# Lengths of k and q from ScalarE's accumulator, and masks made from ScalarE's sign

## The chip, the core and the metric

The kernel runs on one core of a Trainium2 chip. The metric is the device time of one execution in microseconds, as the median of several runs. The core has five engines with a queue of instructions each: TensorE (PE; its weight loads are listed apart as PEld), VectorE (DVE), ScalarE (ACT), GpSimd (POOL) and SyncE (SP, which here issues the DMAs). Each engine takes its instructions strictly in order, and semaphores let one wait for another.

## The reference, cut to what matters

One layer over 1024 tokens of 1024 features: a mixer of two head groups, then an MLP. The change touches two places of the mixer.

The sparse attention keeps, for every query, the 256 keys with the highest score among those it may see, with the earlier key first among equals:

```python
score = jnp.where(key_pos[None, None, :] < limit[None, :, None], score, -jnp.inf)
_, idx = lax.top_k(score, topk)          # topk = 256
```

The DeltaNet group (4 heads of 128) scales every query and key to unit length before its chunked recurrence:

```python
def l2_norm(x):
    return xf * lax.rsqrt(jnp.sum(xf * xf, axis=-1, keepdims=True) + EPS)
q = l2_norm(q.reshape(B, T, B_HEADS, B_HEAD_DIM))
k = l2_norm(k.reshape(B, T, B_HEADS, B_HEAD_DIM))
```

## The kernel before, in words

The program is written as generators (`scoring`, `bisect`, `projections`, `chain`, `levels`, ...) that a planner, `Flow`, interleaves by assumed costs, and the framework's own scheduler then sets the order in which instructions stand in each engine's queue. So an edit in one place can move instructions in others. The stage that matters here lies at about 185 to 427 us of the span. In it run side by side:

- **The projections.** TensorE multiplies the normed input with columns of `w_in` (L199 to L201, the tiles `two`). For q, k and v of the DeltaNet, `conv` follows: a scaled copy on ScalarE (L587), three multiply-adds on VectorE (L589), a Silu on ScalarE (L592).
- **The DeltaNet heads.** When q and k of a head are there, `delta_head` (called four times, for h = 0 to 3) turns them with TensorE (L684, four 128x128 blocks into a PSUM bank, four such banks a head). Of each bank it squares the four blocks (L686 on ScalarE), copies the two of k (L687), and sums the squares per row (L688 on VectorE) into `nr`, a column for every length. From `nr` come the inverse lengths (L691, then the steps L212 to L217) and the factors of the head (L694 to L698); L705 and L706 make the chunk matrices `la`.
- **`base_blocks`.** When the chunk matrices of all heads are stored (`la_d`), this inverts their 32x32 diagonal blocks on VectorE in 31 pairs of steps (L725, L726) and a copy (L727). A store (`tu_d`, L728) and eight loads (`dt`, L740) follow; GpSimd makes `ui` and `te` from `dt` (L783), and the first level of the recurrence goes through TensorE, ScalarE and VectorE (L797, L798, L806, L807, L810, L812, L822, L823, L831, L838, L839).
- **The bisection.** `bisect` finds the threshold of the 256 best scores of each query for six blocks of 128 queries, bit by bit: 31 further bits after the first. In every bit ScalarE counts three blocks (sign and accumulator, L521, widths 1024, 768 and 640), VectorE counts the other three (L528, widths 896, 512 and 384), and VectorE makes the next candidate `cand` of all six from the counts (L531, L532, L533). A sign count of the next bit waits for L533, and L532 waits for the counts of both engines.
- **The masks.** When the thresholds `thr` are there (L540 to L559), each block gets its mask: ScalarE takes the sign of threshold minus score with its sum `sg` (L567), VectorE marks the scores equal to the threshold (L570), counts them along the row (L571, a scan), works out how many are needed (L574, L575), keeps the first of them (L576), adds the greater ones (L577) and writes 0 or a large negative number to `maskb` (L578). The tile `jk`, of two buffers, holds ScalarE's signs and the marks.
- **The end of the stage.** `post_c` scales the latent rows `c_row` (L432 to L437), the last steps of it on VectorE. TensorE turns `c_row` (L1098), and attention and the recurrence begin.

Of the kernel before, what the change touches and what calls it, by code (L numbers as in the profile page):

```python
# [8 lines left out]
F32 = mybir.dt.float32  # L9
F32R = mybir.dt.float32r  # L10
BF16 = mybir.dt.bfloat16
I32 = mybir.dt.int32
AF = mybir.ActivationFunctionType
OP = mybir.AluOpType
AX = mybir.AxisListType
# [3 lines left out]
P = 128  # L19
T = 1024  # L20
# [6 lines left out]
NEG = -2.0 ** 100  # L27
# [112 lines left out]
def block_kernel(ctx: ExitStack, tc: tile.TileContext, x, w_in, c_norm, w_uk, w_uv, rel_bias, conv_w, a_log,  # L140
# [4 lines left out]
    V, S, G, PE, SY = nc.vector, nc.scalar, nc.gpsimd, nc.tensor, nc.sync  # L145
    pl = Pools(tc)
# [141 lines left out]
    ps = psw()  # L288
# [15 lines left out]
    ps = pst()  # L304
# [3 lines left out]
    for half in range(2):  # L308
# [9 lines left out]
        for k in range(NK):  # L318
            ps = psx()
            for j in range(4):  # L320
# [4 lines left out]
                                   op0=OP.mult, op1=OP.subtract)  # L325
# [23 lines left out]
    maskb = pl.t(msk, [P, sum(w_of(b) for b in range(NB))], BF16, "maskb")  # L349
    moff = [sum(w_of(i) for i in range(b)) for b in range(NB)]  # L350
# [14 lines left out]
    ph, ph_close = pl.open("ph")  # L365
# [128 lines left out]
    def bisect():  # L494
        yield "scored"

        cand = pl.t(ph, [P, 6], I32, "cand")
        bare = pl.t(ph, [P, 6], I32, "bare")  # L500
        cnt = pl.t(ph, [P, 6], F32, "cnt")
        lim = pl.t(ph, [P, 6], F32, "lim")
        t01 = pl.t(ph, [P, 6], I32, "t01")
        V.memset(cand, 0)
        for i, b in enumerate(DVB):
            G.memset(lim[:, i:i + 1], P * (b + 1) - TOPK + 0.5)
        for i, b in enumerate(ACB):
            G.memset(lim[:, 3 + i:4 + i], float(P * (b + 1) - 2 * TOPK + 1))


        top = {b: pl.t(ph, [P, P * (b + 1)], BF16, f"top{b}") for b in DVB}
        for b in DVB:
            G.tensor_copy(top[b], s_of(b).bitcast(BF16)[:, 1::2])
        for bit in range(31, -1, -1):
            flip = (1 << bit) ^ (1 << (bit - 1)) if bit else 1
            ta = td = flow.now
            for i, b in enumerate(ACB):
                n = P * (b + 1)
                ta = act(ta, n / 1200 + 0.45)
                junk = pl.t(ph, [P, T], BF16, "jk", bufs=2)  # L520
                S.activation(junk[:, :n], s_of(b), AF.Sign, bias=cand[:, 3 + i:4 + i].bitcast(F32), scale=-1.0,  # L521
                             accum_out=cnt[:, 3 + i:4 + i])
            for i, b in enumerate(DVB):
                n = P * (b + 1)
                td = dve(td, n / 960 + 0.28)
                junk = pl.t(ph, [P, T], BF16, "pre")
                sb = s_of(b) if bit < 16 else top[b]
                V.tensor_scalar(junk[:, :n], sb, cand[:, i:i + 1].bitcast(F32), None, op0=OP.is_lt, op1=OP.add,  # L528
                                accum_out=cnt[:, i:i + 1])
            if bit < 31:  # L530
                V.tensor_scalar(bare, cand, flip, None, op0=OP.bitwise_xor)  # L531
                V.tensor_tensor(t01, cnt, lim, OP.is_le)  # L532
                V.scalar_tensor_tensor(cand, t01, bit, bare, op0=OP.logical_shift_left, op1=OP.bitwise_xor)  # L533
            else:

                V.tensor_tensor(t01, cnt, lim, OP.is_gt)
                V.tensor_scalar(t01, t01, -1.0, None, op0=OP.mult)
                V.tensor_scalar(cand, t01, 1 << 30, None, op0=OP.bitwise_xor)
            yield dve(max(ta, td), 0.8)
        V.tensor_copy(thr[:, 0:3], cand[:, 0:3].bitcast(F32))  # L540


        t = cand[:, 3:6].bitcast(F32)
        up = pl.t(ph, [P, 3], F32, "up")
        least = pl.t(ph, [P, 3], F32, "least")
        for i, b in enumerate(ACB):
            n = P * (b + 1)
            j1 = pl.t(ph, [P, T], BF16, "jk", bufs=2)
            V.tensor_scalar(j1[:, :n], s_of(b), t[:, i:i + 1], None, op0=OP.is_gt, op1=OP.add,
                            accum_out=up[:, i:i + 1])  # L550
            j2 = pl.t(ph, [P, T], BF16, "jk", bufs=2)
            V.tensor_scalar(j2[:, :n], s_of(b), t[:, i:i + 1], BIG, op0=OP.is_le, op1=OP.mult)
            V.tensor_tensor_reduce(out=j2[:, :n], in0=j2[:, :n], in1=s_of(b), scale=1.0, scalar=BIG, op0=OP.add,
                                   op1=OP.min, accum_out=least[:, i:i + 1])
            yield dve(flow.now, 3 * n / 960 + 0.6)
        pick = pl.t(ph, [P, 3], I32, "pick")
        V.tensor_scalar(pick, up, TOPK - 0.5, None, op0=OP.is_ge)
        V.tensor_copy(thr[:, 3:6], t)
        V.copy_predicated(thr[:, 3:6], pick, least)  # L559

        for b in range(NB - 1, 1, -1):
            i = (DVB + ACB).index(b)
            n = P * (b + 1)
            sb, th = s_of(b), thr[:, i:i + 1]
            j1 = pl.t(ph, [P, T], BF16, "jk", bufs=2)
            sg = pl.t(ph, [P, 1], F32, "sg", bufs=2)
            S.activation(j1[:, :n], sb, AF.Sign, bias=th, scale=-1.0, accum_out=sg)  # L567
            eq = pl.t(ph, [P, T], BF16, "jk", bufs=2)
            pre = pl.t(ph, [P, T], mybir.dt.float16, "pre")
            V.tensor_scalar(eq[:, :n], sb, th, None, op0=OP.is_equal)  # L570
            V.tensor_tensor_scan(pre[:, :n], eq[:, :n], eq[:, :n], 0.0, op0=OP.add, op1=OP.max)  # L571

            need = pl.t(ph, [P, 1], F32, "need", bufs=2)
            V.tensor_tensor(need, sg, pre[:, n - 1:n], OP.add)  # L574
            V.tensor_scalar(need, need, 0.5, TOPK - 0.5 * n, op0=OP.mult, op1=OP.add)  # L575
            V.scalar_tensor_tensor(eq[:, :n], pre[:, :n], need, eq[:, :n], op0=OP.is_le, op1=OP.mult)  # L576
            V.scalar_tensor_tensor(eq[:, :n], sb, th, eq[:, :n], op0=OP.is_gt, op1=OP.add)  # L577
            V.tensor_scalar(maskb[:, moff[b]:moff[b] + n], eq[:, :n], -NEG, NEG, op0=OP.mult, op1=OP.add)  # L578
            yield dve(act(flow.now, n / 1200 + 0.4), 5.5 * n / 960 + 1.0)
        flow.done("topk", flow.now)  # L580

# [22 lines left out]
    H4 = [P, 4, P]  # L604

    def v4(ps):
        return ps.rearrange("p (h c) -> p h c", c=P)
# [67 lines left out]
    def delta_head(h, kqh):  # L675

        eh = pl.t(dna, [P, NB, P], F32, "eh")
        SY.dma_start(eh, e_d[h])
        nr = pl.t(dna, [P, NB, 2], F32, "nr")
        kr = pl.t(dna, [P, NB, P], F32, "kr")  # L680
        for n in range(0, NB, 2):
            ps = psx()
            for i in range(4):
                PE.transpose(ps[:, i * P:(i + 1) * P], kqh[:, n + i // 2, i % 2, :], ident)  # L684
            sq = pl.t(dna, H4, F32, "e", bufs=2)
            S.activation(sq, v4(ps), AF.Square)  # L686
            S.copy(kr[:, n:n + 2, :], v4(ps)[:, 0:4:2])  # L687
            V.tensor_reduce(nr[:, n:n + 2, :].rearrange("p n a -> p (n a)"), sq, axis=AX.X, op=OP.add)  # L688
        SY.dma_start(kr_d[:, :, h, :].rearrange("n t d -> t n d"), kr)
        n2 = nr.rearrange("p n a -> p (n a)")  # L690
        V.tensor_scalar(n2, n2, EPS, None, op0=OP.add)  # L691
        r = rsqrt(dna, n2, 16, "rn").rearrange("p (n a) -> p n a", a=2)
        f2 = sm("f2")[:, :, h]
        V.tensor_mul(f2, r[:, :, 0], r[:, :, 0])  # L694
        V.tensor_mul(f2, f2, sm("beta")[:, :, h])
        V.tensor_mul(sm("nk")[:, :, h], nr[:, :, 0], r[:, :, 0])
        V.tensor_mul(sm("k2")[:, :, h], f2, sm("eg")[:, 1, :, h])
        V.tensor_scalar(sm("rq")[:, :, h], r[:, :, 1], 128 ** -0.5, None, op0=OP.mult)  # L698
        for n in range(NB):
            if n % 4 == 0:  # L700
                la = pl.t(dna, [P, 4, 2, P], F32, "la", bufs=2)
            if n % 2 == 0:
                ps = psx()
            o = ps[:, (n % 2) * 256:(n % 2) * 256 + 256]
            PE.matmul(o, kqh[:, n, 0, :], kqh[:, n].rearrange("p a c -> p (a c)"), start=True, stop=True)  # L705
            V.scalar_tensor_tensor(la[:, n % 4], o.rearrange("p (a c) -> p a c", a=2), sm("f2")[:, n, h:h + 1],  # L706
                                   eh[:, n, None, :].to_broadcast([P, 2, P]), op0=OP.mult, op1=OP.mult)
            if n % 4 == 3:
                SY.dma_start(la_d.rearrange("s (n h) a c -> s n h a c", h=4)[:, n - 3:n + 1, h], la)
# [240 lines left out]
    dna = dn = dn2 = at = None  # L950
# [624 lines left out]
    while ready:  # L1575
# [4 lines left out]
        ps = bank_[{2: 1, 3: 5, 4: 7}.get(j, j)]  # L1580
# [225 lines left out]
```

## Time and profile before

| | |
|---|---|
| median of 3 runs | 1376.51 us (1376.21 to 1377.81) |
| profiled execution | 1379.91 us, of which the span is 1378.2 us |
| TensorE busy | 1280.1 us (93%) |
| VectorE busy | 1111.6 us (81%) |
| ScalarE busy | 738.0 us (54%) |
| GpSimd busy | 226.1 us (16%) |
| chain of waits, by engine | PE 66%, DVE 21%, DMA 5%, ACT 4%, issue 2% |

The busy shares are means over stages with different limits. A duration in a timeline runs from the start of an instruction to its end, and the next one on the same engine often starts a little before that end; what an instruction takes of its queue is the distance between two starts. In the chain of waits, "issue" is time in which an engine waited for nothing that the profile shows.

### The profile page before, as it was taken

What the parts mean: (1) busy time and instruction counts of PE and PEld (TensorE: products, weight loads), DVE (VectorE), ACT (ScalarE), POOL (GpSimd) and SP (SyncE); (2) the same over time, 40 slices, a digit from 0 to 9 for tenths busy, and PEclk for the clock granted to TensorE, in tenths of its full rate; (3) what the DMA queues carried; (4) which work ended last, traced back from release to release, by engine and by line L of the source; (5) the groups of instructions that cost most, each with busy time, mean ns of one, the idle gap of its engine ahead of it and who ended that gap; (6) DMA issues with size and microseconds to landing.
All of it is one profiled execution on the core that took longest, in us unless ns stands there. A gap on an engine that the chain in (4) does not pass through costs nothing.

```text
span 1378.2 us, 20181 instructions
## 1 busy us (share of the span) xinstructions
PE 1280.1 (93%) x6628; PEld 1107.6 (80%) x6628; DVE 1111.6 (81%) x2557; ACT 738.0 (54%) x1549; POOL 226.1 (16%) x257
## 2 busy tenths in 40 slices
PE   7899998897977999988989799999999899999996
PEld 5678886776766999978878688888887688888885
DVE  4665679998998899996677467788777978888897
ACT  6555456677614767776455456566656333243422
POOL 1113231221243444349110000000000000000000
PEclk9999999899988999999999999999999999999998
DMA  6223224454255332324455825665567976736215
GB/s 196 78 92 92 62 81 118 137 145 100 69 122 161 95 110 86 95 89 151 152 183 185 295 74 197 213 213 197 202 214 243 393 239 224 248 113 221 78 42 187
DMA packets 184146, 213.33 MB, mean 155 GB/s; under 512 B 28161, under 2 KB 123626, under 8 KB 183914
## 3 DMA queue, kind: packets, MB, share of 16 engines
q1 hardware_dynamic: 184042, 212.06, 47.6%
q8 instruction: 52, 0.85, 0.3%
q14 instruction: 52, 0.43, 0.1%
HBM read 138.58 MB, written 75.00 MB: 155 GB/s over the span
## 4 chain that ended last, share of the span: by engine, by line
PE 66%; DVE 21%; DMA 5%; ACT 4%; issue 2%; SPq 1%; DVEq 0%; ACTq 0%
PE sc L199 4%; PE acc L199 4%; PE sc L200 4%; PE acc L200 4%; PE sc L201 4%; PE acc L201 4%; PE ch L199 4%; PE ch L200 4%; PE ch L201 4%; PE two L199 3%; PE two L200 3%; PE two L201 3%; DVE pre L528 3%; PE tr L199 2%; PE tr L200 2%
## 5 line engine op out<-in xcount | busy, mean ns | idle before, releaser
L199 PE MATMUL two<-hTH,wh 128*128 128x512 f32 (+1 forms) x416 | 166.0, 400 | 22.7 <-ACT tmp L409 14.3
L200 PE MATMUL two<-hTL,wh 128*128 128x512 f32 (+1 forms) x416 | 163.3, 392 | 0.3 <-DVE hTL L324 0.3
L201 PE MATMUL two<-hTH,wl 128*128 128x512 f32 (+1 forms) x416 | 163.0, 393 | 0.0
L521 ACT ACTIVATE jk<-score,cand 128x1024 bf16<-128x1024 f32 (+2 forms) x96 | 92.4, 963 | 52.5 <-DVE cand L533 41.0
L199 PEld LDWEIGHTS two<-hTH,wh 128*128 128x128 f32 (+1 forms) x416 | 80.7, 194 | 39.3 <-issue 18.8
L201 PEld LDWEIGHTS two<-hTH,wl 128*128 128x128 f32 (+1 forms) x416 | 80.9, 194 | 12.9 <-issue 0.5
L200 PEld LDWEIGHTS two<-hTL,wh 128*128 128x128 f32 (+1 forms) x416 | 80.9, 194 | 12.7 <-DVE hTL L324 0.9
L1426 ACT CAST hl<-raw 128x512 fp32r<-128x512 f32 x81 | 48.5, 614 | 70.1 <-PE acc L200 48.7
L1426 ACT CAST hl<-tt 128x512 fp32r<-128x512 f32 x56 | 34.4, 616 | 69.0 <-PE tr L200 39.5
L269 POOL TENSOR_TENSOR wl<-stg,wh 128x1024 fp32r<-128x1024 f32 x23 | 54.7, 2376 | 81.1 <-ACT wh L266 63.7
L1426 ACT CAST hl<-tmp 128x512 fp32r<-128x512 f32 x60 | 35.8, 618 | 55.9 <-DVE tmp L1543 30.3
L1162 ACT ACTIVATE big<-big,nm 128x256 f32<-128x256 f32 (+6 forms) x64 | 50.6, 791 | 22.1 <-DVE nm L1161 18.4
L1427 DVE TENSOR_TENSOR hl<-raw,hl 128x512 fp32r<-128x512 f32 x81 | 55.2, 685 | 5.2 <-ACT hl L1426 2.8
L1188 DVE TENSOR_TENSOR part<-tr,part 128x512 fp32r<-128x512 f32 x80 | 50.3, 631 | 7.3 <-ACT part L1187 7.1
L1210 PE MATMUL acc<-part,VS 128*128 128x256 f32 x288 | 50.0, 297 | 4.1 <-DVE part L1188 4.0
L1187 ACT CAST part<-tr 128x512 fp32r<-128x512 f32 x80 | 42.7, 540 | 16.2 <-PE tr L1185 15.4
L589 DVE SCALAR_TENSOR_TENSOR tmp<-two,svT,tmp 128x1023 f32<-128x1023 f32 (+2 forms) x36 | 45.9, 1276 | 6.3 <-ACT tmp L587 6.3
L199 PE MATMUL acc<-h2H,hl 128*128 128x512 f32 x120 | 46.6, 390 | 3.9 <-ACT tmp L1477 3.9
L479 DVE SCALAR_TENSOR_TENSOR score<-ch,wab,score 128x512 f32<-128x512 f32 (+3 forms) x40 | 26.0, 655 | 28.1 <-ACT ch L478 27.8
L1185 PE MATMUL tr<-ident,big 128*128 128x128 f32 x288 | 46.1, 276 | 2.8 <-DVE part L1188 2.1
L1138 POOL TENSOR_TENSOR mt<-tz,maskb 128x256 f32<-128x256 f32 x56 | 37.9, 682 | 64.0 <-DVE mx L1154 48.3
L268 POOL TENSOR_SCALAR wh<-stg 128x1024 fp32r<-128x1024 f32 x19 | 19.9, 1049 | 170.2 <-PE two L200 156.3
(514 smaller groups left out, 4103.9 us busy)
## 6 DMA issues: line engine op xcount, KB each, us to landing
hid<-tmp SPq DMA_DIRECT2D x140, 256.0 KB, 2.4
hq<-hid SPq DMA_DIRECT2D x80, 256.0 KB, 5.2
raw<-in_w_mlp_in_dram SPq DMA_DIRECT2D x14, 1024.0 KB, 5.7
tmp<-hid SPq DMA_DIRECT2D x56, 256.0 KB, 5.4
raw<-in_w_mlp_out_dram SPq DMA_DIRECT2D x13, 1024.0 KB, 7.4
stg<-in_w_in_dram SPq DMA_DIRECT2D x25, 512.0 KB, 4.0
x<-in_x_dram SPq DMA_DIRECT2D x8, 512.0 KB, 5.4
la_d<-la SPq DMA_DIRECT2D x8, 512.0 KB, 3.0
```

The costliest lines, as they stand in the source:

```text
L199: PE.matmul(o, lh, rh, start=start, stop=False, skip_group_check=more)
L200: PE.matmul(o, lh, rl, start=False, stop=False, skip_group_check=more)
L201: PE.matmul(o, ll, rh, start=False, stop=stop, skip_group_check=more)
L269: (V if early else G).tensor_sub(wl[:, :, :n], f[:, :, :n], wh[:, :, :n].bitcast(F32))
L521: S.activation(junk[:, :n], s_of(b), AF.Sign, bias=cand[:, 3 + i:4 + i].bitcast(F32), scale=-1.0, accum_out=cnt[:, 3 + i:4 + i])
L589: V.scalar_tensor_tensor(acc[:, 3 - j:T], both[:, 0:T - 3 + j], w[j], acc[:, 3 - j:T], op0=OP.mult, op1=OP.add)
L1162: S.activation(pr[:, :n], pr[:, :n], AF.Exp, bias=nm, accum_out=den[:, hh:hh + 1])
L1185: PE.transpose(ps[:, c * P:(c + 1) * P], u["p"][hh][:, (j + a) * P:(j + a + 1) * P], ident)
L1188: V.tensor_sub(pt[:, 0:2 * nj, 1, :], v4(ps)[:, 0:2 * nj], pt[:, 0:2 * nj, 0, :].bitcast(F32))
L1210: PE.matmul(po[:, hh * 256:hh * 256 + 256], VS[:, j + a, 2 * p + hh, :], pt[:, 2 * a + hh].rearrange("p a t -> p (a t)"), start=j + a + hh ...
L1426: S.copy(h_, src)
L1427: eng.tensor_sub(l_, src, h_.bitcast(F32))
```

## The change

In the masks, ScalarE's sign is written into the mask's own place in `maskb` (bf16) instead of a `jk` tile. VectorE's test for equality (L570) and its comparison (L577) read that sign and compare it with the constant 0, where they read the fp32 scores and compared with the threshold of each row.

In `delta_head`, ScalarE squares each 128x128 block in an instruction of its own and sums it per row in its accumulator, straight into `nr`; the wide square and VectorE's reduction go. The copy of k stands ahead of the squares. The new squares are on L688, the copy on L685.

```diff
             n = P * (b + 1)
             sb, th = s_of(b), thr[:, i:i + 1]
-            j1 = pl.t(ph, [P, T], BF16, "jk", bufs=2)
+            mk = maskb[:, moff[b]:moff[b] + n]
             sg = pl.t(ph, [P, 1], F32, "sg", bufs=2)
-            S.activation(j1[:, :n], sb, AF.Sign, bias=th, scale=-1.0, accum_out=sg)
+            S.activation(mk, sb, AF.Sign, bias=th, scale=-1.0, accum_out=sg)
             eq = pl.t(ph, [P, T], BF16, "jk", bufs=2)
             pre = pl.t(ph, [P, T], mybir.dt.float16, "pre")
-            V.tensor_scalar(eq[:, :n], sb, th, None, op0=OP.is_equal)
+            V.tensor_scalar(eq[:, :n], mk, 0.0, None, op0=OP.is_equal)
...
             V.scalar_tensor_tensor(eq[:, :n], pre[:, :n], need, eq[:, :n], op0=OP.is_le, op1=OP.mult)
-            V.scalar_tensor_tensor(eq[:, :n], sb, th, eq[:, :n], op0=OP.is_gt, op1=OP.add)
-            V.tensor_scalar(maskb[:, moff[b]:moff[b] + n], eq[:, :n], -NEG, NEG, op0=OP.mult, op1=OP.add)
+            V.scalar_tensor_tensor(eq[:, :n], mk, 0.0, eq[:, :n], op0=OP.is_lt, op1=OP.add)
+            V.tensor_scalar(mk, eq[:, :n], -NEG, NEG, op0=OP.mult, op1=OP.add)
...
                 PE.transpose(ps[:, i * P:(i + 1) * P], kqh[:, n + i // 2, i % 2, :], ident)
-            sq = pl.t(dna, H4, F32, "e", bufs=2)
-            S.activation(sq, v4(ps), AF.Square)
             S.copy(kr[:, n:n + 2, :], v4(ps)[:, 0:4:2])
-            V.tensor_reduce(nr[:, n:n + 2, :].rearrange("p n a -> p (n a)"), sq, axis=AX.X, op=OP.add)
+            for i in range(4):
+                sq = pl.t(dna, [P, P], BF16, "e", bufs=2)
+                S.activation(sq, ps[:, i * P:(i + 1) * P], AF.Square, accum_out=nr[:, n + i // 2, i % 2:i % 2 + 1])
```

The order of the queues changes with it. The first piece is ScalarE's queue in head 1, before: the sign counts of one bit (L521, to the first of the next bit) with the wide squares (L686, into `e`) and the copies of k (L687).

```order
L521 ACTIVATE jk_2292,cnt_1245<-score_357,cand_1243 128x1024
L521 ACTIVATE jk_2294,cnt_1245<-score_357,cand_1243 128x768
L686 ACTIVATE e_1678<-tr_1673 128x512
L687 COPY kr_1654<-tr_1673 128x256
L521 ACTIVATE jk_2296,cnt_1245<-score_357,cand_1243 128x640
L686 ACTIVATE e_1687<-ch_1682 128x512
L687 COPY kr_1654<-ch_1682 128x256
L521 ACTIVATE jk_2665,cnt_1245<-score_357,cand_1243 128x1024
```

After, ScalarE's queue in the same head, from the last count of one bit to the first of the next, with the narrow squares (L688) between.

```order
L521 ACTIVATE jk_2376,cnt_1245<-score_357,cand_1243 128x640
L688 ACTIVATE e_1695,nr_1673<-ch_1689 128x128
L688 ACTIVATE e_1697,nr_1673<-ch_1689 128x128
L688 ACTIVATE e_1699,nr_1673<-ch_1689 128x128
L688 ACTIVATE e_1701,nr_1673<-ch_1689 128x128
L688 ACTIVATE e_1709,nr_1673<-tr_1703 128x128
L688 ACTIVATE e_1711,nr_1673<-tr_1703 128x128
L688 ACTIVATE e_1713,nr_1673<-tr_1703 128x128
L688 ACTIVATE e_1715,nr_1673<-tr_1703 128x128
L688 ACTIVATE e_1723,nr_1673<-ch_1717 128x128
L688 ACTIVATE e_1725,nr_1673<-ch_1717 128x128
L521 ACTIVATE jk_2745,cnt_1245<-score_357,cand_1243 128x1024
```

Where one wide square stood between two counts, ten narrow ones stand now.

The second place is VectorE's queue at the end of `base_blocks`. Before, its last steps and the copy L727 stand within the last bit of the bisection:

```order
L725 TENSOR_TENSOR kqh_2186<-kqh_2181 128x31
L528 TENSOR_SCALAR pre_3528,cnt_1245<-score_357,cand_1243 128x384
L726 TENSOR_TENSOR kqh_2181<-kqh_2181,kqh_2186 128x31
L532 TENSOR_TENSOR t_207_1247<-cnt_1245,lim_1246 128x6
L727 COPY kqh_2181<-kqh_2181 128x1024
L533 SCALAR_TENSOR_TENSOR cand_1243<-t_207_1247,bare_1244 128x6
```

After, VectorE's queue has them within the second mask (that of width 896):

```order
L725 TENSOR_TENSOR kqh_2266<-kqh_2261 128x31
L570 TENSOR_SCALAR jk_3661<-maskb_340 128x768
L575 TENSOR_SCALAR need_3653<-need_3653 128x1
L726 TENSOR_TENSOR kqh_2261<-kqh_2261,kqh_2266 128x31
L576 SCALAR_TENSOR_TENSOR jk_3649<-pre_3650,need_3653,jk_3649 128x896
L727 COPY kqh_2261<-kqh_2261 128x1024
L577 SCALAR_TENSOR_TENSOR jk_3649<-maskb_340,jk_3649 128x896
```

The copy moved from ahead of the last threshold to behind the first mask and half of the second.

The third place is VectorE's queue where the first level of the recurrence stands. Before, L807 stands among the masks:

```order
L570 TENSOR_SCALAR jk_3597<-score_357,thr_365 128x640
L807 TENSOR_SCALAR te_2707<-ch_2850 32x4x32
L577 SCALAR_TENSOR_TENSOR jk_3584<-score_357,thr_365,jk_3584 128x768
L571 SCALAR_TENSOR_TENSOR pre_3598<-jk_3597 128x640
L578 TENSOR_SCALAR maskb_340<-jk_3584 128x768
```

After, VectorE's queue has the whole level and the scaling of `c_row` (from L434) behind the last mask:

```order
L577 SCALAR_TENSOR_TENSOR jk_3697<-maskb_340,jk_3697 128x384
L578 TENSOR_SCALAR maskb_340<-jk_3697 128x384
L807 TENSOR_SCALAR te_2787<-ch_2930 32x4x32
L812 TENSOR_SCALAR ui_2785<-ch_2930 32x4x32 x2
L831 TENSOR_TENSOR vk_2786<-ch_2971,sm_nk_1502 128x512
L839 TENSOR_SCALAR ui_2785<-ch_3040 64x4x64
L434 TENSOR_SCALAR css_2986<-css_2986 128x8
L212 TENSOR_SCALAR cr_u_3009<-css_2986 128x8
```

The level's four steps moved from between the masks to behind them all.

## Rows read from the trace of the kernel before

**Rows 1.** Busy us and instructions by engine in three stretches; PEclk is the granted clock.

```profile
185.00:310.00 125.00, 114.03 (x520) 96.29 (x519) 118.11 (x309) 84.85 (x163) 29.72 (x22) 0.95 0.45 128
310.00:375.00 65.00, 55.09 (x243) 46.54 (x242) 60.74 (x177) 44.47 (x97) 17.17 (x10) 0.95 0.30 78
375.00:425.00 50.00, 34.22 (x167) 28.35 (x165) 48.46 (x82) 11.87 (x31) 17.72 (x11) 0.82 0.55 134
```

**Rows 2.** Waits from 180 to 425 us: total us, times, longest.

```profile
ACT jk L521 <- DVE cand L533: 41.0, 24, 4.1
...
DVE t L532 <- ACT jk L521: 1.8, 6, 0.5
```

**Rows 3.** Timeline in head 0: start us, us, engine, line, operation.

```profile
187.51 0.59 ACT L686 ACTIVATE e<-tr 128x512 f32<-128x512 f32 x1
187.99 0.38 ACT L687 COPY kr<-tr 128x256 f32<-128x256 f32 x1
...
188.17 0.68 DVE L688 TENSOR_REDUCE nr<-e 128x4 f32<-128x512 f32 x1
188.76 0.74 DVE L528 TENSOR_SCALAR_CACHE_REDUCE pre<-top,cand 128x512 bf16<-128x512 bf16 x1
```

**Rows 4.** Narrow squares elsewhere: timeline (PSUM), and groups with mean ns (SBUF).

```profile
416.44 0.28 ACT L432 ACTIVATE c_row<-ch 128x128 f32<-128x128 f32 x1 [0.28 <-PE ch L429]
...
416.71 0.27 ACT L432 ACTIVATE c_row<-ch 128x128 f32<-128x128 f32 x1
...
L927 ACT ACTIVATE sq<-o 128x128 bf16<-128x128 f32 x32 | 9.6, 302 | 4.1 <-DVE o L907 2.1 <-DVE o L909 1.9
L927 ACT ACTIVATION_READ_ACCUMULATOR sq<-o 128x1 f32 x32 | 6.0, 189 | 0.0
```

**Rows 5.** One bit of the bisection in the timeline; two groups of VectorE.

```profile
197.79 1.15 ACT L521 ACTIVATE jk<-score,cand 128x1024 bf16<-128x1024 f32 x1 [3.66 <-DVE cand L538]
...
200.58 0.19 ACT L521 ACTIVATION_READ_ACCUMULATOR jk<-score,cand 128x1 f32 x1
...
202.36 2.38 POOL L269 TENSOR_TENSOR wl<-stg,wh 128x1024 fp32r<-128x1024 f32 x1
...
202.42 2.34 DVE L533 SCALAR_TENSOR_TENSOR cand<-t,bare 128x6 int32<-128x6 int32 x1
...
L528 DVE TENSOR_SCALAR_CACHE_REDUCE pre<-score,cand 128x896 bf16<-128x896 f32 (+2 forms) x48 | 39.8, 829 | 0.2
...
L726 DVE TENSOR_TENSOR kqh<-kqh,kqh 128x31 f32<-128x31 f32 (+15 forms) x31 | 12.2, 392 | 0.1
```

**Rows 6.** The masks on VectorE in the timeline.

```profile
384.33 0.75 DVE L570 TENSOR_SCALAR jk<-score,thr 128x1024 bf16<-128x1024 f32 x1
385.12 2.29 DVE L571 TENSOR_TENSOR_SCAN pre<-jk 128x1024 f16<-128x1024 bf16 x1
...
401.11 0.61 DVE L570 TENSOR_SCALAR jk<-score,thr 128x768 bf16<-128x768 f32 x1
...
405.02 1.02 DVE L576 SCALAR_TENSOR_TENSOR jk<-pre,need,jk 128x768 bf16<-128x768 f16 x1
...
406.85 1.02 DVE L577 SCALAR_TENSOR_TENSOR jk<-score,thr,jk 128x768 bf16<-128x768 f32 x1
...
409.19 0.33 DVE L578 TENSOR_SCALAR maskb<-jk 128x768 bf16<-128x768 bf16 x1
```

**Rows 7.** Timeline from the end of `base_blocks` to the end of the stage.

```profile
375.19 1.08 DVE L727 COPY kqh<-kqh 128x1024 f32<-128x1024 f32 x1
376.19 0.15 DVE L533 SCALAR_TENSOR_TENSOR cand<-t,bare 128x6 int32<-128x6 int32 x1
...
386.00 5.91 POOL L783 TENSOR_TENSOR ui<-dt,bd 128x512 f32<-128x512 f32 x3 [19.67 <-DMA dt<-tu_d]
...
393.30 1.97 PE L797 MATMUL ch<-te,lo 128*128 128x64 f32 x8 [3.59 <-POOL te L783]
...
426.71 1.97 PE L1098 MATMUL tr<-ident,c_row 128*128 128x128 f32 x8 [6.53 <-DVE c_row L437]
```

## The prediction

> **What bounds the kernel now.** I read three views, in this order. The table of stretches comes first: between 185 and 425 us the reader sees VectorE busy for 118.1 of 125 us, then 60.7 of 65, then 48.5 of 50, while ScalarE is busy for 84.9, 44.5 and 11.9 and TensorE for 114.0, 55.1 and 34.2 [rows 1]. Both edits of this change lie in these 240 us. VectorE has 12.7 us without work in them. Then the waits of the same stretch: ScalarE stood idle 41.0 us for VectorE's next threshold (L533), and VectorE only 1.8 us for ScalarE's counts (L532) [rows 2]. So VectorE sets the pace, and the loop between the two engines is not closed tightly. Last, the end of the stage: TensorE stands still until c_row is written by VectorE (L437) and starts the attention part at 426.71 [rows 7]. I call that moment the stage's end. I take what moves it to move the program's end by as much, since nothing later can begin without it.
>
> The frame: the profiled execution took 1379.91 us (a span of 1378.2 and 1.7 around it), 3.4 above the median of 1376.51. I sum differences within the trace and apply them to the median.
>
> **The change part by part.**
>
> *The reductions that go.* Sixteen of them, 0.68 us each; one started at 188.17 and the next instruction on VectorE at 188.76, so each takes 0.59 us of the queue [rows 3]. 16 x 0.59 = 9.4 us: 2.4 in head 0, which lies ahead of the bisection's first threshold, and 7.1 in heads 1 to 3.
>
> *The squares that come.* A wide square took 0.48 us of ScalarE's queue (187.51 to 187.99 [rows 3]); four narrow ones with an accumulator replace it. The trace has no such operation in this place, but two like it: on a 128x128 block of PSUM the next one started 0.27 us later (416.44, 416.71), and from SBUF one takes 0.30 and its accumulator 0.19 [rows 4], which overlap to about 0.30 a pair. I take 0.28, near the PSUM one, since the new squares read PSUM, and keep 0.27 to 0.33 for the range. 64 x 0.28 - 16 x 0.48 = 17.9 - 7.7 = 10.2 us more for ScalarE. By the stretches alone ScalarE has that room. The question is whether it has it at the right places.
>
> *The places: round by round.* The bisection has 31 bits. In each ScalarE runs three sign counts, 2.98 us from the first start to the last accumulator (197.79 to 200.77 [rows 5]), and VectorE three counts (mean 0.83) and three small steps, some 2.8 us net of overlaps [rows 5]; neither can start the next bit without the other. What else stands in either queue within a round is read from the order. I priced every round so, each instruction at the spacing of its rows, and took the longer queue. Before, ScalarE's is the longer in 6 of 30 rounds, by 3.8 us in all. After, it is in 11, by 14.8 us: squares stand in bundles between two counts, up to 12 in a round (one such piece is shown above: 10 squares, 2.8 us, after a count, and the next count behind them), and the heads' later steps (L691 on) fall behind, so that VectorE's queue holds rounds of almost nothing but counts in between. VectorE's own sum falls from 158.1 to 144.1: 7.1 for the reductions, and the rest for steps of base_blocks that now stand behind the last bit: 17 steps at about 0.32 (rows of 0.39 less an overlap of 0.08 [rows 5]) and the copy L727 (1.0), 6.4 us in all. So the longer queues sum to 158.1 + 3.8 = 161.9 before and 144.1 + 14.8 = 158.9 after: the last bit ends 3.0 us earlier, not 14. Head 0 adds about 1.0: it loses 2.4 on VectorE, but the conv's copy (L587) now waits behind two more narrow squares on ScalarE, and VectorE waits for that. Both orders pay as well for GpSimd: L533 at 202.42 took 2.34 us and ended with GpSimd's L269, 202.36 to 204.74 [rows 5]. There are 13 such pairs, and I leave them equal. So the last threshold, 376.34 before [rows 7], comes at 372.3.
>
> *The masks.* The equality test read fp32 scores: 0.61 us at 768 columns. A tensor_scalar from bf16 to bf16 at that width took 0.33 (L578) [rows 6]. Scaled over the six widths (4224 columns) that saves 0.28 x 4224 / 768 = 1.5 us. The comparison L577 keeps its time: L576, whose operands have 16 bits each, took 1.02 us at 768 columns, as L577 with fp32 did [rows 6]. The test now waits for ScalarE's sign of its block (1.15 us and an accumulator), where it read the scores at once. For the first block that is covered: six steps of base_blocks (1.9 us) stand between the thresholds (L559) and the test; without them it would cost 1.3. The later signs no longer wait for a buffer of "jk" and come a block ahead, so I cost them at nothing; what is queued behind a late test would be all of VectorE.
>
> *The end of the stage.* This is where the order moves most. Before, base_blocks is finished (L727, 375.19) ahead of the masks, and its store, the loads of dt, GpSimd's products (from 386.00) and TensorE's L797 at 393.30 run beside them [rows 7]; 17.0 us lie between L727's end and L797. After, L727 stands behind one and a half masks, and the level's steps (L807, L812, L831, L839) and the whole scaling of c_row stand behind the last mask. From the last threshold, then: 8.0 us to the masks as before (376.34 to 384.33 [rows 6]), 6.4 for the base_blocks steps, 10.2 for the mask instructions ahead of L727 (the scan of 2.29 at 1024 and 2.0 at 896, two STT at 1.2 and one at 1.1, and small ones [rows 6]), 17.0 to L797, and 12.2 from there to c_row. The last is my estimate: three hops between TensorE, ScalarE and VectorE to L807 (3.4, with L797's 1.97 at half clock), four more to L839 (4.0), and twelve steps of about 0.19 and two of 1.23 for c_row (4.8). In all 53.8 us, against 426.71 - 376.34 = 50.4 before. The way through the masks (8.0 + 6.4 + 24.8 + 6.5 of waiting for GpSimd, as before, + 8.8) comes to 54.5, about as long.
>
> **Sum:** the last threshold 4.0 earlier, the rest 3.4 longer: -0.6 us. 1376.5 - 0.6 = 1375.9, no change that can be told: 0.2% is 2.75 us, and a measurement here tells no less.
>
> **Rivals.**
>
> *VectorE stays the bound.* If ScalarE's bundles cost nothing, the last threshold comes 7.1 + 2.4 + 6.4 = 15.9 earlier and the stage's end 15.9 - 3.4 = 12.5 earlier: 1364. For it speaks that ScalarE waited 41 us for VectorE [rows 2], and that part of its surplus falls together with VectorE's waits for GpSimd. Against it: the bundles stand in front of counts. Half of it (six of the eleven rounds free) gives 1369. The Trainium skill ("Perfetto Trace Analysis", Optimizing Scalar/DVE Operations) says that with a saturated VectorE it may make sense to move work to ScalarE, and also that larger operations give more throughput; by its first sentence the time would be this rival's, and the rows bear out the saturation [rows 1], not that ScalarE is free when it matters.
>
> *The late base_blocks decides.* If the squares take 0.33 each, ScalarE's surplus grows by 64 x 0.05 = 3.2 us, nearly all of the 4.0 is gone, and the 3.4 us by which the chain L727, dt, L783, L797, c_row is now longer stand alone: 1379.3. With 2 us of waits for GpSimd on the small steps of c_row as well, it is 1381. It decides from the point where the last threshold comes less than 0.7 us earlier. For it: 17 us of this chain are DMA and GpSimd, which no shorter VectorE shortens [rows 7].
>
> *The tests are not faster.* If bf16 brings nothing, 1.5 us are lost on the way through the masks: 1377.4, still no change.
>
> **How the numbers follow.** The forecast, within 0.2%: 0.40. The first rival, whole or in part: 0.33. The second: 0.27. The third falls within the first. The range 1367 to 1382 leaves out a whole first rival (0.10) and the worst of the second (0.08). The likeliest case alone spans 1373.8 to 1379.3. Beyond the stage the order differs too, in the attention part; I know no sign for that, and it widens both sides by about 2.
>
> **What would show it.** Right: VectorE waits for ScalarE at L532 some 10 us or more in 185 to 375, where it was 1.8; the last L533 ends near 372; L797 starts 17 us after L727's end and within 2 us of the last mask; TensorE restarts on c_row near 426. Wrong: few waits at L532 and a last threshold near 361 (first rival); narrow squares spaced over 0.33 us, or TensorE idle ahead of L797 with all masks long done (second). Were the tests still at 0.6 us for 768 columns, the third would hold. What makes it wrong at large is a wrong price of the hops at the end, each of which I have only from other places.

## The result, and the profile after

The changed kernel takes 1386.53 us (median of 6 runs, 1383.99 to 1393.29), the kernel before on the same chip 1375.72: a ratio of 1.0082, with a 95% interval of 1.0061 to 1.0102. It is slower by about 11 us, and the forecast of 1375.9 (1367 to 1382) was wrong. The runs of one kernel spread over some 10 us here, so differences below 2 us don't show in times. The profiled execution of after took 1384.87 us (span 1383.2), only 5.0 more than that of before, because the latter lay 4.2 us above its own median and the former 1.7 below. One pair of profiles therefore doesn't carry the whole difference. Verdicts below go by medians.

The stretches of [rows 1], after (us, busy by engine, then the granted clock):

```profile
185.00:310.00 125.00, 119.39 (x569) 102.28 (x567) 107.93 (x286) 97.03 (x284) 33.24 (x24) 0.99 0.44 127
310.00:375.00 65.00, 55.44 (x235) 46.94 (x235) 59.46 (x176) 41.98 (x91) 13.71 (x8) 0.92 0.33 90
375.00:425.00 50.00, 26.39 (x132) 22.87 (x130) 44.40 (x89) 9.77 (x26) 11.64 (x9) 0.70 0.50 122
```

VectorE lost 11.5 us of work in the first two stretches and ScalarE gained 9.7, as the edits say. In the third TensorE is busy for 26.4 us where it was for 34.2, and its granted clock fell from 0.82 to 0.70. The waits from 180 to 430 us (total, times, longest):

```profile
ACT jk L521 <- DVE cand L533: 40.2, 20, 5.8
...
PE ch L797 <- POOL te L783: 19.4, 1, 19.4
...
DVE t L532 <- ACT jk L521: 6.6, 5, 2.4
```

Beside [rows 2], VectorE now waits 6.6 us for ScalarE's counts, and TensorE stands 19.4 us ahead of L797 (3.6 before, [rows 7]). From the last threshold to the end of the stage, in the timeline (start, us, engine, line):

```profile
372.23 0.16 DVE L533 SCALAR_TENSOR_TENSOR cand<-t,bare 128x6 int32<-128x6 int32 x1
...
383.00 0.43 DVE L570 TENSOR_SCALAR jk<-maskb 128x1024 bf16<-128x1024 bf16 x1
...
393.27 1.03 DVE L727 COPY kqh<-kqh 128x1024 f32<-128x1024 f32 x1
```

```profile
409.95 1.97 PE L797 MATMUL ch<-te,lo 128*128 128x64 f32 x8 [19.37 <-POOL te L783]
...
412.70 1.92 PE L806 MATMUL ch<-y,ui 128*128 128x32 f32 x8 [0.79 <-ACT y L798]
...
416.19 0.26 DVE L578 TENSOR_SCALAR maskb<-jk 128x384 bf16<-128x384 bf16 x1
416.48 0.28 DVE L807 TENSOR_SCALAR te<-ch 32x128 f32<-32x128 f32 x1
...
420.61 1.06 PE L429 MATMUL ch<-ident,tmp 128*128 128x128 f32 x4
...
423.10 0.15 DVE L434 TENSOR_SCALAR css<-css 128x8 f32<-128x8 f32 x1
...
425.38 1.26 POOL L783 TENSOR_TENSOR ui<-dt,bd 128x512 f32<-128x512 f32 x1 [4.52 <-PE ch L870]
425.57 2.15 DVE L436 TENSOR_TENSOR c_row<-c_row,cr_y 128x1024 f32<-128x1024 f32 x1
426.61 1.97 POOL L783 TENSOR_TENSOR te<-dt,bd 128x384 f32<-128x384 f32 x1
427.76 1.90 DVE L437 TENSOR_TENSOR c_row<-c_row,cn_b 128x1024 f32<-128x1024 f32 x1
429.71 1.11 PE L1098 MATMUL tr<-ident,c_row 128*128 128x128 f32 x4 [4.41 <-DVE c_row L437]
```

The last threshold comes 4 us earlier, L727 18 us later, L1098 3.0 us later than in [rows 7]. One pair of profiles is a weak measure of the first and the last of these. The runs below give four profiles with the front of before (the front is all that stands in the queues up to L1098): the last L533 starts there at 373.2 to 378.4 us and L1098 at 423.4 to 429.0. In three with the front of after they start at 372.2 to 375.6 and at 429.7 to 432.8. By the means the threshold comes some 2 us earlier and L1098 some 5 us later. What hardly scatters is the way from the one to the other: 50.1 to 50.7 us before, 57.2 to 57.5 after. So the stage's end explains some 3 to 5 of 11 us. The experiments look for the rest.

### The profile page after: what moved, and what is told of

Read it like the earlier page. It is cut to its first block, busy times and chain, and to the rows that moved or that the text cites. A ratio compares the mean times of both kernels' runs of the same rounds, so it can differ in the third digit from the quotient of the medians.

```text
span 1383.2 us, 20266 instructions
## 1 busy us (share of the span) xinstructions
PE 1284.8 (93%) x6628; PEld 1110.8 (80%) x6628; DVE 1097.4 (79%) x2541; ACT 748.0 (54%) x1661; POOL 222.5 (16%) x257
## 5 line engine op out<-in xcount | busy, mean ns | idle before, releaser
L201 PE MATMUL two<-hTH,wl 128*128 128x512 f32 (+1 forms) x416 | 162.1, 390 | 0.0
L521 ACT ACTIVATE jk<-score,cand 128x1024 bf16<-128x1024 f32 (+2 forms) x96 | 93.0, 971 | 42.4 <-DVE cand L533 40.2
L201 PEld LDWEIGHTS two<-hTH,wl 128*128 128x128 f32 (+1 forms) x416 | 79.8, 192 | 12.5 <-issue 0.7
L1210 PE MATMUL acc<-part,VS 128*128 128x256 f32 x288 | 52.3, 303 | 0.5 <-DVE part L1188 0.3
L199 PE MATMUL acc<-h2H,hl 128*128 128x512 f32 x120 | 46.3, 387 | 2.0 <-ACT tmp L1477 2.0
L199 PE MATMUL sc<-hl,hq 128*128 128x512 f32 x112 | 43.0, 384 | 3.9 <-DMA hq<-hid 1.9
L201 PE MATMUL acc<-h2H,hl 128*128 128x512 f32 x120 | 46.5, 387 | 0.0
```

Of the source, the lines that this page charges most:

```text
L199: PE.matmul(o, lh, rh, start=start, stop=False, skip_group_check=more)
L201: PE.matmul(o, ll, rh, start=False, stop=stop, skip_group_check=more)
L1210: PE.matmul(po[:, hh * 256:hh * 256 + 256], VS[:, j + a, 2 * p + hh, :], pt[:, 2 * a + hh].rearrange("p a t -> p (a t)"), start=j + a + hh ...
```

## Experiments

Theory A: the narrow squares delay the heads, base_blocks ends behind the masks, and the chain from L727 to c_row costs the time. Rivals: the masks' edit costs it (C); or the loss lies behind the stage, in the order of the instructions that the scheduler chose there (B, later D and E). In the tables of medians, "before" is the kernel before on the same chip.

### Each edit alone

`lengths_alone` has the `delta_head` hunk only, `masks_alone` the `bisect` hunk only.

> The kernel before with the edit in delta_head alone (narrow squares with accumulators, no reduction); the masks compare scores as before. Theory A (late chain): the squares delay the heads, base_blocks ends behind the masks, L797 waits for it, and c_row (L429, L432, L437) stands behind L797's level in TensorE's queue; then this edit carries the whole loss: 1386 to 1389 us, TensorE idle for 15 us or more ahead of L797 and a granted clock near 0.7 in 375 to 425. Rival C (the masks' tests, now waiting for ScalarE's sign, cost the time): within 2 us of the kernel before, 1374 to 1378.

> The kernel before with the edit in the masks alone. Theory A: the queues up to the masks are those of before, so L727 and L797 stay within 1 us of 375 and 393, and the time is 0 to 2 us below before, 1374 to 1376. Rival C: slower by 5 us or more, 1381 to 1387, with VectorE waiting for ScalarE's sign at L570.

Measured: lengths_alone 1385.84 (ratio 1.0063, 1.0038 to 1.0088), masks_alone 1383.75 (1.0048, 1.0027 to 1.0068). The first fits theory A: TensorE is idle for 22.45 us ahead of L797, at a granted clock of 0.73 from 375 to 425. The second lies in the range of rival C, but without its sign: VectorE waits for ScalarE's sign at L570 only once, for 1.3 us. L1098 starts at the early end of the profiles with the front of before, and the program still ends later:

```profile
423.77 1.97 PE L1098 MATMUL tr<-ident,c_row 128*128 128x128 f32 x8 [4.69 <-DVE c_row L437]
```

Each edit alone costs more than half of what both cost together. Such costs don't add up, which speaks against either edit's own work as the whole cause. One thing more can be read off the traces: behind the stage every engine's queue in masks_alone stands in exactly the order of after.

### The row that ties c_row to the late level

In both kernels `post_c`'s second half takes a PSUM bank of the ring `ch`, so L429 stands behind the recurrence's level in TensorE's queue. The edit, on after and on before:

```diff
         for hf in range(2):
-            ps = psx()
+            ps = pst()
```

> The changed kernel, with both halves of post_c in banks of the ring tr, where the second half took a bank of ch, the ring of the recurrence's levels (L424, psx becomes pst). The steps of c_row (L434 to L437) then stand among the bits of the bisection and L1098 ahead of L797. Theory A: TensorE works on attention while L797 waits, the gap of 19.4 us ahead of L797 falls below 10, and 5 to 15 us are gained on the changed kernel: 1371 to 1381. Rival B (the loss lies in the order of the attention part and not at the stage's end): 1383 to 1388 as before this edit, whatever the gap.

> The kernel before with the same edit of post_c. The masks of before end at 421.7 and c_row at 426.7, so by theory A at most 5 us are to be had at the stage's end, 1370 to 1376, and the distance to the changed kernel with the same edit falls from 11 to within 5. By rival B the distance between the two stays near 11.

Measured: 1374.89 on after (0.9993, 0.9975 to 1.0010) and 1377.24 on before (1.0008, 0.9983 to 1.0033), which is 1 us above the range that theory A gave. All 11 us come back on after, as theory A said, but not in its way. L1098 starts at 375.20, and the gap ahead of L797 stays at 17.3 us:

```profile
415.51 1.97 PE L797 MATMUL ch<-te,lo 128*128 128x64 f32 x8 [17.31 <-POOL te L783]
```

The edit also gave everything behind it another order. That left B open, and the next four runs take it up.

### The masks' edit, split by what it does to the order

`test_alone` reads the sign in L570 only, `comparison_alone` in L577 only (both write the sign into `maskb`). The first leaves the queues behind the stage as they were, the second puts them in an order that is neither that of before nor that of after, though L577 takes about the same time on either operand (0.96 us at 768 columns after, 1.02 before).

```diff
-            V.tensor_scalar(eq[:, :n], sb, th, None, op0=OP.is_equal)
+            V.tensor_scalar(eq[:, :n], mk, 0.0, None, op0=OP.is_equal)
```

```diff
-            V.scalar_tensor_tensor(eq[:, :n], sb, th, eq[:, :n], op0=OP.is_gt, op1=OP.add)
+            V.scalar_tensor_tensor(eq[:, :n], mk, 0.0, eq[:, :n], op0=OP.is_lt, op1=OP.add)
```

> The kernel before with ScalarE's sign in the mask's place and only the test for equality (L570) reading it; the comparison L577 reads the scores as before. This leaves TensorE's queue as it was but for one pair of instructions, and VectorE's but for places among the masks, so it shows the faster test without another order behind the stage. Theory D (the order of the attention part, which moved with the masks' edit, cost masks_alone its 7 us): 1374 to 1377, the kernel before or a little below. Rival C (the masks themselves cost, by the wait for the sign or by the sign standing in maskb): 1381 to 1387 like masks_alone.

> The kernel before with ScalarE's sign in the mask's place and only the comparison L577 reading it; L570 reads the scores as before. L577 takes the same time on either operand, so nothing in this kernel is faster or slower by more than 0.3 us, but the queues behind the stage stand in another order (590 of TensorE's rows differ from before). Theory D: the time moves by 2 us or more from before, as the order falls, in either direction; the stage's end stays within 1 us of 426.7. Rival C, or no effect of orders: 1375 to 1378.

Measured: test_alone 1375.94 (0.9996, 0.9979 to 1.0014), comparison_alone 1385.17 (1.0063, 1.0038 to 1.0088). The line that saves work is worth nothing that can be told, and the line that changes no work costs 9 us. Its stage ends at 428.40, later than the 426.7 forecast by 1.7 us but within the scatter of the profiles with the front of before. Rival C falls, theory D stands.

### Head 3 as before

```diff
+            if h in (3,): sq = pl.t(dna, H4, F32, "e", bufs=2); S.activation(sq, v4(ps), AF.Square); S.copy(kr[:, n:n + 2, :], v4(ps)[:, 0:4:2]); V.tensor_reduce(nr[:, n:n + 2, :].rearrange("p n a -> p (n a)"), sq, axis=AX.X, op=OP.add); continue
             S.copy(kr[:, n:n + 2, :], v4(ps)[:, 0:4:2])
```

`head3_test_crow` has this, test_alone's masks and the bank of `tr` for c_row.

> The changed kernel, but head 3 takes its lengths as before (a wide square and VectorE's reduction); heads 0 to 2 keep the narrow squares. In the changed kernel head 3's sixteen squares stood one or two at a time between sign counts, from 285 to 300. Theory A: base_blocks ends ahead of the last threshold again (L727 near 375), L797 starts near 395, TensorE keeps the projections to fill its waits, the gap ahead of L797 is below 6, and 3 to 6 us come back at the stage's end: 1378 to 1384, depending on the order behind it. Rival B (nothing of the loss is at the stage's end): 1385 to 1389.

> Three things together on the changed kernel: head 3 as before, L577 reading the scores, and post_c's second half in a bank of tr. Theory A: L727 ahead of the last threshold, c_row ready among the bits, so that L1098 starts well ahead of L797's level, and attention waits for masks alone: 1366 to 1374, below both kernels. Rival B or D (the order behind decides): anywhere from 1372 to 1384.

Measured: head3_reduced 1378.72 (1.0023, 1.0005 to 1.0041). L797 is back at 392.44, behind a gap of 2.7 us, and L1098 at 424.73, 2 us ahead of [rows 7]. So the late chain was head 3's doing, as theory A said. But the kernel is still not faster than before. head3_test_crow: 1371.00 (0.9961, 0.9947 to 0.9974), faster than both kernels.

### The order pinned

The decisive pair. Behind the stage both kernels have the same instructions, so the order of one can be forced on the other. A table holds, for each engine, the places of all instructions behind the stage (from L1098 on TensorE, behind L437 on VectorE) in the wanted order, and each gets an order edge, without a semaphore, to the one ahead of it:

```diff
         block_kernel(tc, *args)
+        _pin(nc, tc, _mybir)
...
+    for e, s in tab:
...
+        for a, b in zip(row, row[1:]):
+            tc.add_manual_dep(b, a.name, mb.DependencyInfo(mb.DependencyClass.NoSync, mb.DependencyReason.DATA), reason="order")
```

`after_old_order` is the changed kernel up to the stage's end and the order of before behind it; `before_new_order` the converse; `head3_test_old_order` is head3_reduced with test_alone's masks and the order of before.

> The changed kernel up to the stage's end, with every engine's instructions behind it pinned to the order that they have in the kernel before (from L1098 on TensorE, behind L437 on VectorE, and likewise on ScalarE, GpSimd and the DMA queue). Theory E (two parts: the late chain at the stage's end, and the order that the scheduler chose behind it): only the first part is left, 2 to 3 us at the stage's end and up to 2 us of half clock behind it, so 1378 to 1380, and the stretch from L437 to the last L1388 is within 2 us of the 340.8 of before. Rival B' (the late stage's end is the whole loss): 1384 to 1388.

> The converse: the kernel before up to the stage's end, with the order that the changed kernel has behind it. Nothing that the change computes is in it. Theory E: the second part alone, 4 to 8 us slower than before: 1380 to 1384, and L437 to the last L1388 longer by as much. Rival B': 1375 to 1378, as before.

> The changed kernel itself once more, beside the three on the same chip. 1384 to 1388 by all theories; by E its distance to the kernel before is the sum of the distances of after_old_order and before_new_order within 3 us, and its stretch from L437 to the last L1388 is again longer than before's by 2 to 6 us.

> The changed kernel with head 3 as before and L577 reading the scores, pinned behind the stage to the order of before. head3_reduced ended its stage at 424.7 by its trace and lost it behind (1378.7). Theory E: with the order of before the gain at the stage's end stays: 1373 to 1375.5. Rival F (the gain at the stage's end is given back behind it whatever the order, for instance to the clock): 1376 to 1380.

| kernel | front | order behind | median us | ratio to before (95%) |
|---|---|---|---|---|
| before | before | before | 1376.29 | 1 |
| after_old_order | after | before | 1378.08 | 1.0024 (1.0004 to 1.0043) |
| before_new_order | before | after | 1385.41 | 1.0068 (1.0049 to 1.0088) |
| after_again | after | after | 1387.51 | 1.0082 (1.0060 to 1.0104) |
| head3_test_old_order | head 3 as before | before | 1371.52 | 0.9966 (0.9953 to 0.9979) |

The two parts are 0.24% and 0.68%, and together 0.92% beside the 0.82% of the whole: theory E. Its numbers were less exact: before_new_order came out 1.4 us above its range. L437 to the last L1388 took 336.9 us in after_old_order, 4 below the 340.8 expected, 346.7 in before_new_order, within its range, and 349.3 in after_again, 8.5 more than before where 2 to 6 were expected. In the traces the compute queues behind the stage stand in the wanted order. The pinning itself is not what costs: after_old_order is pinned too, and masks_alone has the order of after without it. Of 11 us some 9 are the order behind the stage, which has nothing to do with lengths or masks, and some 2 or 3 are the late end of the stage. With the order held, a front that ends 2.6 us earlier (L1098 at 424.13) is 4.7 us faster, more than was expected; rival F falls.

### Which part of the order

Both are the kernel before. What belongs to attention, recurrence and output projection is pinned to one kernel's order, the MLP to the other's.

> The kernel before, pinned behind the stage: what belongs to attention, recurrence and output projection (all that is written ahead of L1470) in the order that the changed kernel has, the MLP in the order of before. Theory G (the attention part holds it): 1383 to 1387, with the waits of L1233 for L1229 (3.9 us in the changed kernel, none before) in the trace. Rival H (the MLP's order holds it): 1375 to 1378.

> The converse: attention, recurrence and output projection in the order of before, the MLP in that of the changed kernel. Theory G: 1375 to 1378. Rival H: 1382 to 1387.

Measured: before_attention_order 1384.76 (1.0060, 1.0040 to 1.0079), before_mlp_order 1371.80 (0.9981, 0.9961 to 1.0000). It is the attention part (theory G). Which of its moved instructions, and which engine's queue, makes the difference stays open. TensorE's waits in that stretch, first in the order of before (before_mlp_order), then in that of after (before_attention_order):

```profile
PE acc L1210 <- DVE part L1188: 3.6, 5, 1.7
PE tr L1185 <- DVE part L1188: 2.2, 3, 1.5
```

```profile
PE acc L1233 <- DVE ol L1229: 3.9, 3, 1.8
...
PE ch L201 <- DVE ol L1308: 3.2, 1, 3.2
PE ch L199 <- ACT oh L1307: 1.4, 2, 0.7
PE ch L830 <- issue: 1.2, 1, 1.2
```

The waits are other ones, few and short. What follows them is dearer. The same two stretches in before_mlp_order and in before_attention_order:

```profile
500.00:620.00 120.00, 114.49 (x925) 106.08 (x925) 110.07 (x431) 86.08 (x241) 48.73 (x60) 1.00 0.32 96
620.00:690.00 70.00, 67.53 (x406) 60.43 (x404) 50.72 (x181) 39.34 (x101) 34.65 (x31) 1.00 0.51 162
```

```profile
500.00:620.00 120.00, 113.80 (x883) 104.76 (x882) 106.62 (x414) 82.84 (x232) 44.02 (x57) 0.96 0.30 88
620.00:690.00 70.00, 63.77 (x370) 55.73 (x369) 50.58 (x189) 37.23 (x96) 34.35 (x31) 0.95 0.44 144
```

TensorE is busy for nearly as long from 500 to 620 and gets 42 instructions fewer done (not all of the same kinds, as the orders differ), at a clock of 0.96. Three waits of before_attention_order, and windows of 2 us around the last two:

```profile
529.72 1.09 PE L830 MATMUL ch<-ident,in 128*128 128x128 f32 x4 [1.17 <-issue]
...
604.98 1.12 PE L1233 MATMUL acc<-fold,ol 128*128 128x64 f32 x4 [1.84 <-DVE ol L1229]
...
653.28 0.79 PE L201 MATMUL ch<-wh,ol 128*128 128x512 f32 x1 [3.20 <-DVE ol L1308]
```

```profile
602.00:604.00 2.00, 0.78 (x6) 0.53 (x5) 1.91 (x8) 1.98 (x7) 0.00 (x0) 1.00 0.26 74
604.00:606.00 2.00, 1.02 (x5) 1.03 (x6) 1.97 (x6) 1.04 (x2) 0.00 (x0) 0.64 0.30 90
606.00:608.00 2.00, 2.00 (x11) 2.00 (x11) 1.94 (x6) 0.00 (x0) 0.00 (x0) 0.50 0.00 0
608.00:610.00 2.00, 2.00 (x11) 2.00 (x10) 0.55 (x2) 0.94 (x2) 0.00 (x0) 0.50 0.00 0
...
652.00:654.00 2.00, 0.72 (x2) 0.63 (x3) 2.00 (x4) 0.00 (x0) 0.69 (x1) 0.58 0.11 33
654.00:656.00 2.00, 2.00 (x6) 1.55 (x5) 0.82 (x2) 0.00 (x0) 0.00 (x0) 0.50 0.73 219
```

Towards the end of each wait the granted clock falls to 0.50 (1.2 instead of 2.4 GHz) and stays there for 3.4 us at the first and 6.8 at the others. Not every wait does this: in before_mlp_order TensorE stood 1.70 us ahead of an L1210 at 604.35 and kept 1.00. The stretch from the first L1098 to the last L1388 in the profiles, with TensorE's idle time and the time at the lower clock (summed from windows of 2 us):

| order of the attention part | kernels | stretch us | idle us | at 0.50, us |
|---|---|---|---|---|
| before | before, test_alone, before_mlp_order, after_old_order, head3_test_old_order, head3_test_mlp_order | 335.0 to 339.5, mean 336.8 | 13.2 | 9.8 |
| after | after, after_again, before_new_order, before_attention_order, masks_alone | 340.9 to 349.2, mean 345.6 | 16.2 | 17.8 |
| others | lengths_alone, head3_reduced, comparison_alone | 342.9 to 349.7 | 14.0 to 18.6 | 15.2 to 24.6 |

Of the 8.8 us between the first two means, 3.0 are waits and about 4 (half of 8.0 more at the lower clock, an estimate) the clock; the rest I can't place. The profiled execution of after (340.9) happened to be a short one, with 9.5 us at the lower clock; after_again has the same order, nearly the same waits (3.6 us ahead of L201 where after had 1.4) and 23.4.

### Two attempts to gain more

`best_old_order` pins head3_test_crow from its first logits on to the order of before; `head3_test_mlp_order` is head3_test_old_order with the MLP in the order of after.

> head3_test_crow (1371.0) with the order of before from the first logits (L1147 on TensorE, L1154 on VectorE, L1162 on ScalarE) on. If its own order costs as the changed kernel's does: 1363 to 1368. If its own order is as good as that of before, which its stretch to the last L1388 speaks for (760.1, before 766.2): 1369 to 1373.

> head3_test_old_order (head 3 as before, L577 reading the scores, attention in the order of before) with the MLP in the order of the changed kernel. If that order is worth the 3.5 us that before_mlp_order showed: 1367 to 1369. If the 3.5 us were scatter: 1371 to 1373.

Measured: best_old_order 1379.77 (1.0031, 1.0014 to 1.0047), 0.7% above the same kernel with its own order. Neither range held it. So the order of before is not good in itself: it did well behind three fronts here (before, after, head 3 as before) and not behind this one. The traces say in part where the time went: from the first L1147 to the last L1388 best_old_order takes 329.1 us and head3_test_crow 317.1, with 20.5 and 3.4 us at the lower clock. Half of the difference, 8.5 us by estimate, is most of the 12. Why the waits fall so is not shown. head3_test_mlp_order: 1370.21 (0.9962, 0.9945 to 0.9979), against 0.9966 with the MLP's old order. It lies between the two ranges expected. So the MLP's order is worth nothing that can be told here, and before_mlp_order's 3.5 us, which lay below its range too, was probably scatter in the main. head3_test_crow, head3_test_old_order and head3_test_mlp_order are all 0.34 to 0.39% faster than the kernel before.

## Why the prediction was wrong

**The frame failed first.** "I take what moves it to move the program's end by as much" is the step that cost most. before_new_order has the front of before and ends some 9 us later. I had written that the order differs beyond the stage, knew no sign, and gave it 2 us on either side without a row for that size. It was 0.68%, some 9 us, in before_new_order. None of my rivals held it, so the range ended below the time.

**VectorE's and ScalarE's share** was nearly right. The reductions are gone (107.9 and 59.5 us busy against [rows 1]). The squares took 0.26 of the queue each, not 0.28, head 3's among them:

```profile
285.18 0.27 ACT L688 ACTIVATE e<-tr 128x128 bf16<-128x128 f32 x1
285.34 0.19 ACT L688 ACTIVATION_READ_ACCUMULATOR e<-tr 128x1 f32 x1
285.44 0.27 ACT L688 ACTIVATE e<-tr 128x128 bf16<-128x128 f32 x1
```

The last threshold ended at 372.39, forecast 372.3. That hit is luck in part: by the seven profiles named with the result it came some 2 us earlier than before, not 4.0. VectorE's waits at L532 came to 6.6 us and not to 10 or more, so the way to that number was less exact too. (Within it, VectorE's own sum fell by 14.0, and the parts named for that make 13.5.) The first rival (a threshold near 361) was rightly put second: moving work off a busy VectorE shortened its loop by far less than the work moved. The Trainium skill ("Perfetto Trace Analysis", Optimizing Scalar/DVE Operations) says that such a move may make sense when VectorE is saturated; here VectorE was saturated [rows 1], and of the 15.9 us that the first rival counted on 4 came in this pair of profiles and some 2 by the means. The Trainium skill says in the same section that larger operations can improve throughput if the engine is saturated. ScalarE was not, with 97.03 of 125 us busy, but the direction agrees: sixteen wide squares of 0.48 us became 64 narrow ones of 0.26.

**Why base_blocks was late** the prediction took from the order, without its reason. Head 3's squares stood one to three at a time between sign counts, from 285.18 to 300.79, and L691 waited for the last of them:

```profile
300.82 0.17 DVE L691 TENSOR_SCALAR nr<-nr 128x16 f32<-128x16 f32 x1 [0.82 <-ACT e L688]
```

Before, it had started at 294.34. head3_reduced shows that this head alone makes the lateness.

**The masks**: L570 took 0.36 us at 768 columns (0.61 in [rows 6]) and L577 did not change, as forecast; the third rival falls.

```profile
391.75 0.36 DVE L570 TENSOR_SCALAR jk<-maskb 128x768 bf16<-128x768 bf16 x1
...
398.84 0.96 DVE L577 SCALAR_TENSOR_TENSOR jk<-maskb,jk 128x768 bf16<-128x768 bf16 x1
```

**The end of the stage** was forecast at 53.8 us behind the last threshold and took 57.3 (372.39 to 429.71). Up to L727's end it took 21.9 (24.6 forecast), from there to L797 15.7 (17.0), and from L797 to L1098 19.8 where I had put 12.2. That last term, which I had called my estimate, is the mis-sized one. Of its two ways the sum also took the shorter, 53.8, where by its own figures the longer, 54.5, would decide. L807 started at 416.48, right behind the last mask and not behind L806, which ended at 414.62: the way through the masks decided, and its tail, put at 8.8, took 13.2. Half of that, 6.6 us, is the level's hops and c_row's squares up to L434, with TensorE at half clock (L822 1.97) and L429 behind L822 and L830 in its queue. The other half is c_row, with L436 and L437 at 2.15 and 1.90 where I had 1.23 each. The Trainium skill ("SBUF — State Buffer", Who interferes with whom) says that a VectorE instruction with two inputs in SBUF and a GpSimd instruction that reads SBUF exclude each other. The rows agree: L436 and L437 each end 1.08 us after a product of GpSimd's L783 does (426.64 to 427.72, and 428.58 to 429.66). Of the signs named, L797 within 2 us of the last mask did not show: it started 6.5 us ahead of that mask's end.

**The second rival** named this chain and its sign, and priced it at 1379.3 to 1381. (1376.5 + 3.4 makes 1379.9, so its lower price is a little low.) The front's part, 1378.1 in after_old_order, is near it, but by luck: its condition did not come true. The squares took 0.26 and not 0.33, and the threshold came earlier by more than 0.7 us. The chain became longer at its tail instead. The other 9 us it did not hold either.

## What to carry to other kernels

Where a scheduler orders the queues from a simulated time, every edit is two edits: its own work, and a new order of everything behind it. Price the second, or hold it fixed with order edges, before you read the first from a time; an edit that changes no work is the control that shows how much the order is worth. When work moves to an engine with room, look whether the last item of the chain (here head 3) is still on time, not only whether the sums fit.

## What I had not expected of the hardware

Waits of 1.17 to 3.20 us on TensorE in a dense stretch went with 3.4 to 6.8 us at half clock; the one of 1.84 so cost about 3.4 us more (half of 6.8, an estimate). Between profiles of one kernel such intervals came and went: 9.5 and 23.4 us at the lower clock in two profiles of the changed kernel, whose waits ahead of L1233 were 3.9 us in both. What decides it these runs don't show. At the stage's end the clock of after was at 0.50 from 394.9 to 432.4 us; TensorE had been idle from 390.6 on. Before, there were three such intervals of 7, 7 and 10 us between 393 and 431.
